# Attention's gating products and their lower pieces, moved from VectorE to GpSimd

## The chip, the cores and the metric

The kernel runs on one core of one Trainium2 chip. A core has five engines, each with its own instruction queue that it works off in order: TensorE (PE in the profile; its weight loads are PEld) multiplies matrices into PSUM, VectorE (DVE) and ScalarE (ACT) do element-wise work, GpSimd (POOL) does element-wise work on SBUF, and SyncE (SP) issues DMA transfers; ScalarE and GpSimd issue some of them too. [...] The metric is the time of one execution on the device, in microseconds (us); lower is better.

## What is computed

A decoder trunk of two layers on 1024 tokens of width 1024, in float32. Each layer normalises x, projects it to 5376 columns, runs two token mixers side by side, merges them by sigmoid gates and adds the projected result to x:

```python
h = rms_norm(x, norm_w[layer])
proj = h @ w_in[layer]
(q, k, v, z_attn, q_h, f_h, i_h, g_h, gate_attn, gate_hgrn) = jnp.split(proj, split_points, axis=-1)
...
a = sliding_window_attention(q, k, v, attn_sinks[layer]).astype(x.dtype) * jax.nn.silu(z_attn)
...
o = hgrn2_recurrence(heads(qin), heads(kin), heads(i_h.astype(jnp.float32)), heads(logf))
...
merged = (jax.nn.sigmoid(gate_attn) * (a @ w_up_attn[layer])
          + jax.nn.sigmoid(gate_hgrn) * (b @ w_up_hgrn[layer]))
x = x + merged @ w_out[layer]
```

The change concerns the product `* jax.nn.silu(z_attn)` in the line of `a`, and the preparation of `a` for `a @ w_up_attn`.

## The kernel before

Large matrix products are made in three: an operand is split into an upper piece, which is the value rounded to the matmul format fp32r, and a lower piece, which is what the rounding left. ScalarE makes the upper piece with a cast, and VectorE subtracts it from the value to get the lower piece. `split_w` does this into tiles that are used in turn, `split_slot` into tiles of the large pool (lines 380 to 385: the cast is L383, the subtraction L384). `split_w` already has an argument that names the engine of the subtraction; at the start of the kernel it is GpSimd for one chunk of weights.

A layer runs in stages. First come the projections in pairs (`pair`), then attention by blocks of 128 queries with the value projections of the recurrence beside it. Attention's output goes to DRAM (`ad`), and so does silu of its gate (`zd`). Then comes the stage of the heads, around which this case turns. The recurrence has four heads, and each is a generator (`core`) of ten steps: products that double a range (`grow`, with L946 on the query side Q and L955 on the key side R, both on VectorE), small matmuls into PSUM (`lv` L992 and L933, `l` L1044 and L1050, `lv_m` L1057), VectorE's merging of these into `acc`, GpSimd's copies of `acc` into the score tile `scT` (L1070), transposes (`tn` L1080), the states (`kv` L1092, then a chain of VectorE updates of R, L1096 and L1098) and the output (`po` L1109 and L1111). ScalarE copies the output to `tab` (L1112) and sums its squares (L1114), VectorE turns these sums into a scale (`ms_o` L116 and the lines up to L130) and applies it (L1116). `finish_head` transposes the result (`tb` L1125), multiplies it by its gate and splits it.

Between the steps of the heads the loop at the end of the stage advances a second generator, `filling`. It has TensorE project the forget gates and queries of heads 1 to 3 (`pj_f`, `pj_qh`), two chunks of weights a head, in halves, and then the upper projection of attention, `up_attn` (`pu_ua`, lines 147 to 149). After the halves 6, 7, 8 and 9 it calls `gate_attn`, once for each quarter of `a` (two halves of the tokens by two pairs of 128 channels). One call loads a quarter of the gate (`zr`) and of attention's output (`ar` in the profile) from DRAM with two DMAs on SyncE's queue (L1139), multiplies them on VectorE (L1140), and splits the product: cast on ScalarE (L383, `wh_a`), subtraction on VectorE (L384, `wl_a`). `up_attn` uses all four quarters as moving operands. SyncE's queue also holds the loads of weights (`wr`, `wr_ua`), which wait until one of three buffers comes free, and those of the heads (`f`, `R`, `Q`).

The order of the instructions in each engine's queue is not the order of the text. A planner sets it when the kernel is built: it estimates when each instruction's operands are ready, and fills each engine with what is ready first, by the place in the text among several. So a projection may stand between two steps of a head, and an instruction may be set at the head of a queue before its operand has in fact arrived, because the planner took the transfer to be done sooner. A few edges (`keep_in_program_order`, `issue_after`) tie the order elsewhere; none lies in this stage.

Of the kernel before, what the change touches and what calls it, by code (L numbers as in the profile page):

```python
# [10 lines left out]
F32 = mybir.dt.float32  # L11
# [3 lines left out]
ALU = mybir.AluOpType  # L15
AX = mybir.AxisListType

P = 128
# [22 lines left out]
def trunk_kernel(ctx, tc, x, positions, norm_w, w_in, attn_sinks, hgrn_norm_w, w_up_attn,  # L41
# [3 lines left out]
    V, S, G, PE = nc.vector, nc.scalar, nc.gpsimd, nc.tensor  # L45
# [11 lines left out]
    def slot(shape, name, dt=F32):  # L57
        return sp.tile(shape, dt, tag="slot", name=name)
# [318 lines left out]
        wh, wl = chunk(w, c0, nm)  # L377
        colsA(wh, wl, hT, nm, use, [H0, H1])

    def split_slot(raw, nm, shape):  # L380
        hi = slot(shape, f"wh_{nm}", F32R)
        lo = slot(shape, f"wl_{nm}", F32R)
        S.copy(hi, raw)  # L383
        V.tensor_tensor(out=lo, in0=raw, in1=hi.bitcast(F32), op=ALU.subtract)  # L384
        return hi, lo

    def split_rows(w, c0, n, nm, first=0):


        g = 1024 // n  # L390
        res = {}
        for k in range(0, KT, g):
            raw = wp.tile([P, g, n], F32, tag="wraw", name=f"wr_{nm}_{k}", bufs=3)
            nc.sync.dma_start(raw, w[k * P:(k + g) * P, c0:c0 + n].rearrange("(k p) c -> p k c", p=P))
            hi, lo = (split_w if k < first else split_slot)(raw, f"{nm}_{k}", [P, g, n])
            for j in range(g):
                res[k + j] = (hi[:, j], lo[:, j])
        return res
# [121 lines left out]
    for L in range(DEPTH):  # L520
# [54 lines left out]
        if L == 0:  # L575
            hT, hF = HT("0"), Turned("0")
            rest = norm_turn_soon([y for b in range(2) for y in norm_scale(xns[b:b + 1], None, f"n0_{b}", False, True)],
                                  hT, hF, 0, "n0_0", wt)
            aw = [split_w(raws[j], f"p0_{j}", [P, KT, P], G if j else V) for j in range(2)]
            aw += [split_slot(raws[j], f"p0_{j}", [P, KT, P]) for j in range(2, 4)]  # L580
            ys = list(norm_scale(xns[2:4], wb, "n0_2", True))
            for j in range(4):
# [275 lines left out]
        for u in range(NB):  # L858
            before(u)
            value(u)  # L860
            attend(u)
            if u == 5:
                w = [split_slot(load_chunk(wi, OF, f"f{L}_0"), f"f{L}_0", [P, KT, P])]
# [269 lines left out]
        def gate_attn(asp):  # L1133

            a = 0 if len(asp[0]) < 2 else 1
            j = len(asp[a])
            zr, t = (slot([P, 2, 512], f"{n}r_{L}_{a}_{j}") for n in ("z", "a"))
            for d, src in ((zr, zd), (t, ad)):
                nc.sync.dma_start(d, src[:, 2 * j:2 * j + 2, a * 512:(a + 1) * 512])  # L1139
            V.tensor_tensor(out=t, in0=t, in1=zr, op=ALU.mult)  # L1140
            asp[a].append(split_slot(t, f"a{L}_{a}_{j}", [P, 2, 512]))

        def filling():

            asp = [[], []]
            n = 0
            for h in range(1, NHG):
                for do, c in ((forget, OF), (query, OQH)):
                    w = chunk(wi, c + h * P, f"{c}_{L}_{h}")
                    for half in (H0, H1):  # L1150
                        do(h, w, [half])
                        yield
                        n += 1
                        if n in GATE:
                            gate_attn(asp)
            for m in range(0, KT, 2):
                for _ in up_attn(m, asp):
                    yield
# [35 lines left out]
        for m in range(0, KT, 2):  # L1194
# [5 lines left out]
            for a in range(2):  # L1200
                u, t = u2s[m // 2][a]
# [166 lines left out]
```

## Time and profile before

| what | value |
|---|---|
| time of the runs, median (lowest to highest of 3) | 1387.02 us (1384.45 to 1387.6) |
| the profiled execution's own time | 1387.23 us |
| its span on the core | 1385.5 us |
| TensorE busy | 98% of the span |
| VectorE, ScalarE, GpSimd busy | 72%, 51%, 8% |
| granted TensorE clock, mean | 0.996 |

The stage of the heads with its filling lies at about 430 to 575 us of the span for layer 0 and at about 1107 to 1256 us for layer 1.

The views are read as follows. A row of a group has the line, the engine, the operation, the tile written and the tiles read, the shapes and the count; in the view of a tile, the smallest, median and largest duration in ns and the first and last start. A row of the timeline has the start in us from the start of the span, the duration in us, the engine and the instruction; in brackets stands how long the engine sat idle before it and what ended that. Durations on one engine overlap slightly, since the next instruction starts while the last one drains. A row of the waits has the waiting engine and line, the one it waited for, the total in us, the count and the longest. A row of the stretches has start and end, length, busy time of PE, PEld, DVE, ACT and POOL with their instructions, the granted TensorE clock, the DMA engines' share and GB/s. Ends of matmuls are modelled, and spans on GpSimd are rough.

### The profile page before, as it was taken

To read this page: it belongs to the slowest core of one execution; us is meant where nothing else is said; L and a number is where in the kernel's file an instruction comes from. 1 tells how busy PE (TensorE), PEld (TensorE's weight loads), DVE (VectorE), ACT (ScalarE), POOL (GpSimd) and SP (SyncE) were. 2 spreads that over 40 slices of the span, in tenths; PEclk is the share of its full clock that TensorE was granted. 3 is DMA by queue.
4 is the path that set the end of the run, shared out by engine and by line. 5 is a ranking of instruction groups with operands and counts; after the bars stand their busy time and mean duration, and the time that the engine had idled before them with its cause. 6 is when DMAs were issued, how large, how long until landed. Compare 5 with 4: busy or idle time off the path is not lost.

```text
span 1385.5 us, 21538 instructions
## 1 busy us (share of the span) xinstructions
PE 1356.9 (98%) x8236; PEld 1127.0 (81%) x8236; DVE 997.3 (72%) x1638; ACT 708.8 (51%) x1418; POOL 109.2 (8%) x195
## 2 busy tenths in 40 slices
PE   7999999999999999999999999999999999999997
PEld 7888888888877888888888888887887788788885
DVE  6867668843646898599959666776356487867998
ACT  8844333443786655323666333344367766352254
POOL 1100012320000001000000001222100000100000
PEclk9999999999999999999999999999999999999999
DMA  9444476875225652860256336587913476329203
GB/s 290 165 134 145 137 225 204 264 262 212 92 95 189 231 189 76 310 239 29 86 181 189 126 125 194 173 259 217 335 49 107 142 236 217 108 85 402 91 1 122
DMA packets 204279, 240.06 MB, mean 173 GB/s; under 512 B 14288, under 2 KB 140752, under 8 KB 204176
## 3 DMA queue, kind: packets, MB, share of 16 engines
q1 hardware_dynamic: 156528, 145.08, 32.0%
q10 hardware_dynamic: 34944, 52.44, 10.4%
q0 software_dynamic: 12704, 41.17, 9.3%
q8 instruction: 65, 1.06, 0.3%
q14 instruction: 38, 0.31, 0.1%
HBM read 160.00 MB, written 78.64 MB: 172 GB/s over the span
## 4 chain that ended last, share of the span: by engine, by line
PE 80%; DVE 13%; ACT 3%; DMA 2%; issue 2%; SPq 0%; DVEq 0%; ACTq 0%
PE pb L308 6%; PE pb L310 6%; PE pb L309 6%; PE pc L308 4%; PE pc L310 4%; PE pc L309 4%; PE pg L270 3%; PE pg L272 3%; PE pg L271 3%; PE pu_uh L149 2%; PE pu_uh L147 2%; PE pu_uh L148 2%; PE pi L843 2%; PE pi L842 2%; PE pi L844 2%; PE av L816 2%
## 5 line engine op out<-in xcount | busy, mean ns | idle before, releaser
L136 ACT CAST whi_s<-ws 128x1024 fp32r<-128x1024 f32 x30 | 31.6, 1054 | 90.4 <-PE pc L310 89.0
L319 DVE TENSOR_TENSOR pq<-pc,pq 128x512 f32<-128x512 f32 x37 | 25.6, 691 | 61.4 <-PE pc L310 56.2
L136 ACT CAST whi_o<-wo 128x1024 fp32r<-128x1024 f32 x20 | 21.1, 1054 | 78.7 <-PE pu_uh L149 35.5
L544 ACT ACTIVATE pq<-pq 128x512 f32<-128x512 f32 x60 | 37.9, 631 | 43.9 <-DVE pq L319 42.3
L136 ACT CAST whi_t<-ws 128x1024 fp32r<-128x1024 f32 x30 | 31.6, 1054 | 41.8 <-PE pc L310 27.9
L147 PE MATMUL pu_ua<-wh_a,wlo_ua 128*128 128x512 f32 x128 | 52.2, 408 | 0.0
L780 ACT ACTIVATE pr<-pr,mx 128x128 f32<-128x128 f32 x128 | 49.6, 391 | 4.1 <-DVE mx L777 3.7
L149 PE MATMUL pu_ua<-wh_a,whi_ua 128*128 128x512 f32 x128 | 51.0, 399 | 0.0
L148 PE MATMUL pu_ua<-wl_a,whi_ua 128*128 128x512 f32 x128 | 50.3, 393 | 0.0
L147 PE MATMUL pu_uh<-wh_b,wlo_uh 128*128 128x512 f32 x128 | 49.8, 389 | 0.0
L148 PE MATMUL pu_uh<-wl_b,whi_uh 128*128 128x512 f32 x128 | 49.8, 389 | 0.0
L149 PE MATMUL pu_uh<-wh_b,whi_uh 128*128 128x512 f32 x128 | 49.8, 389 | 0.0
L270 PE MATMUL pg<-hh,wl_p 128*128 128x512 f32 (+1 forms) x128 | 46.9, 368 | 1.0 <-DVE wl_p L384 1.0
L308 PE MATMUL pb<-th,wl 128*128 128x512 f32 x120 | 47.2, 393 | 0.5 <-ACT pq L349 0.4
L308 PE MATMUL pb<-th,wlo_s 128*128 128x512 f32 x120 | 47.1, 392 | 0.0
L308 PE MATMUL pc<-hh,wlo_t 128*128 128x512 f32 x120 | 46.8, 390 | 0.0
L310 PE MATMUL pb<-th,wh 128*128 128x512 f32 x120 | 46.7, 389 | 0.0
L309 PE MATMUL pb<-tl,wh 128*128 128x512 f32 x120 | 46.7, 389 | 0.0
L310 PE MATMUL pc<-hh,whi_t 128*128 128x512 f32 x120 | 46.7, 389 | 0.0
L309 PE MATMUL pc<-hl,whi_t 128*128 128x512 f32 x120 | 46.7, 389 | 0.0
L310 PE MATMUL pb<-th,whi_s 128*128 128x512 f32 x120 | 46.7, 389 | 0.0
L309 PE MATMUL pb<-tl,whi_s 128*128 128x512 f32 x120 | 46.7, 389 | 0.0
(432 smaller groups left out, 4447.4 us busy)
## 6 DMA issues: line engine op xcount, KB each, us to landing
wr<-in_w_in_dram SPq DMA_DIRECT2D x72, 512.0 KB, 4.6
gd<-pq ACTq DMA_DIRECT2D x79, 256.0 KB, 3.0
fq<-fq ACTq DMA_DIRECT2D x48, 256.0 KB, 2.7
wr_p<-in_w_in_dram SPq DMA_DIRECT2D x23, 512.0 KB, 5.6
x<-in_x_dram SPq DMA_DIRECT2D x16, 512.0 KB, 6.3
qs<-qsd POOLq DMA_DIRECT2D x16, 512.0 KB, 7.5
u<-gd SPq DMA_DIRECT2D x16, 512.0 KB, 10.1
ga<-gd SPq DMA_DIRECT2D x16, 512.0 KB, 10.3
```

What stands on the lines that cost most here:

```text
L136: S.copy(hi, raw)
L147: PE.matmul(acc, lhsT=ll, rhs=rh, start=i == 0, stop=False)
L148: PE.matmul(acc, lhsT=lh, rhs=rl, start=False, stop=False)
L149: PE.matmul(acc, lhsT=lh, rhs=rh, start=False, stop=i == n - 1)
L270: PE.matmul(acc, lhsT=wl[:, k], rhs=h[:, t], start=k == 0, stop=False, skip_group_check=q > 0)
L271: PE.matmul(acc, lhsT=wh[:, k], rhs=l[:, t], start=False, stop=False, skip_group_check=q > 0)
L272: PE.matmul(acc, lhsT=wh[:, k], rhs=h[:, t], start=False, stop=k % 4 == 3, skip_group_check=q > 0)
L308: PE.matmul(acc, lhsT=wl[:, k], rhs=h, start=start and k == 0, stop=False, skip_group_check=not start)
L309: PE.matmul(acc, lhsT=wh[:, k], rhs=l, start=False, stop=False, skip_group_check=not start)
L310: PE.matmul(acc, lhsT=wh[:, k], rhs=h, start=False, stop=k == 3, skip_group_check=not start)
L544: S.activation(d, src, AF.Sigmoid if r < 2 * KT else AF.Silu)
L780: S.activation(pr[:, h], pr[:, h], AF.Exp, bias=mx[:, h:h + 1], accum_out=sm[:, h:h + 1])
```

## The change

`split_slot` gets an argument that names the engine of its subtraction, VectorE unless said otherwise. In `gate_attn` the product and the subtraction are given to GpSimd (`G`); `V` is VectorE and `S` ScalarE. The cast between them stays on ScalarE and the loads stay on SyncE. Eight products and eight subtractions are concerned, four of each in a layer. The other callers of `split_slot` are as before.

```diff
-    def split_slot(raw, nm, shape):
+    def split_slot(raw, nm, shape, eng=V):
         hi = slot(shape, f"wh_{nm}", F32R)
         lo = slot(shape, f"wl_{nm}", F32R)
         S.copy(hi, raw)
-        V.tensor_tensor(out=lo, in0=raw, in1=hi.bitcast(F32), op=ALU.subtract)
+        eng.tensor_tensor(out=lo, in0=raw, in1=hi.bitcast(F32), op=ALU.subtract)
         return hi, lo
...
             for d, src in ((zr, zd), (t, ad)):
                 nc.sync.dma_start(d, src[:, 2 * j:2 * j + 2, a * 512:(a + 1) * 512])
-            V.tensor_tensor(out=t, in0=t, in1=zr, op=ALU.mult)
-            asp[a].append(split_slot(t, f"a{L}_{a}_{j}", [P, 2, 512]))
+            G.tensor_tensor(out=t, in0=t, in1=zr, op=ALU.mult)
+            asp[a].append(split_slot(t, f"a{L}_{a}_{j}", [P, 2, 512], G))
```

## The prediction

> **What bounds the kernel now.** I read the page first: the engines' busy time and the list of the costliest groups. TensorE (PE) is busy 98% of the span, VectorE (DVE) 72%, GpSimd (POOL) 8%.
>
> ```profile
> span 1385.5 us, 21538 instructions
> PE 1356.9 (98%) x8236; PEld 1127.0 (81%) x8236; DVE 997.3 (72%) x1638; ACT 708.8 (51%) x1418; POOL 109.2 (8%) x195
> ```
>
> The profiled execution took 1387.23 us by its own clock, 1.73 us more than its span and 0.21 us above the median of 1387.02. I make the sum against 1387.23. A kernel that is 98% TensorE can gain only where TensorE waits, so the next view was that of TensorE's waits. Its largest row is the wait of the `lv` products (L992) for the doubling step of R (L955):
>
> ```profile
> PE lv L992 <- DVE R L955: 5.8, 2, 3.8
> PE tb L1125 <- DVE tab L1116: 3.4, 6, 0.9
> ```
>
> It is 5.8 us in two places, one in each layer. The timeline of TensorE gives both places, with the idle time ahead of them in brackets, and the `l` products (L1044) some 15 us earlier, which the chain below starts from:
>
> ```profile
> 477.91 0.39 PE L1111 MATMUL po<-R,Q 128*128 128x128 f32 x2
> 483.71 1.02 PE L1044 MATMUL l<-Q,R 128*32 128x64 f32 x29
> 501.38 0.64 PE L992 MATMUL lv<-f,ones 128*32 128x256 f32 x8 [2.07 <-DVE R L955]
> ...
> 1160.78 1.02 PE L1044 MATMUL l<-Q,R 128*32 128x64 f32 x29
> ```
> ```profile
> 1175.97 0.40 PE L148 MATMUL pu_ua<-wl_a,whi_ua 128*128 128x512 f32 x1
> 1180.14 1.08 PE L992 MATMUL lv<-f,ones 128*32 128x256 f32 x8 [3.77 <-DVE R L955]
> ```
>
> What TensorE waits for is VectorE, and VectorE had itself been standing still. Its timeline in layer 0, then in layer 1:
>
> ```profile
> 474.97 1.21 DVE L137 TENSOR_TENSOR wlo<-wr,whi 128x1024 fp32r<-128x1024 f32 x1
> 476.11 0.34 DVE L1098 SCALAR_TENSOR_TENSOR R<-R,tab,kv 128x128 f32<-128x128 f32 x1
> 483.59 1.23 DVE L1140 TENSOR_TENSOR ar<-ar,zr 128x1024 f32<-128x1024 f32 x1 [6.01 <-DMA ar<-ad]
> 485.93 1.22 DVE L384 TENSOR_TENSOR wl_a<-ar,wh_a 128x1024 fp32r<-128x1024 f32 x1 [1.11 <-ACT wh_a L383]
> 487.07 0.16 DVE L116 TENSOR_SCALAR ms_o<-so 128x8 f32<-128x8 f32 x1
> ...
> 500.63 0.69 DVE L955 TENSOR_TENSOR R<-R,tab 128x512 f32<-128x512 f32 x1
> ```
> ```profile
> 1162.36 1.23 DVE L1140 TENSOR_TENSOR ar<-ar,zr 128x1024 f32<-128x1024 f32 x1 [7.62 <-DMA ar<-ad]
> 1165.84 0.17 DVE L116 TENSOR_SCALAR ms_o<-so 128x8 f32<-128x8 f32 x1
> ...
> 1179.39 0.69 DVE L955 TENSOR_TENSOR R<-R,tab 128x512 f32<-128x512 f32 x1
> ```
>
> The fourth gating product (L1140) of each layer stands at the head of VectorE's queue for 6.01 and 7.62 us until its load lands. Then come the lower piece (L384) and a chain without a gap, from `ms_o` to the end of the R that TensorE waits for: 487.07 to 501.32 in layer 0 (14.25 us), 1165.84 to 1180.08 in layer 1 (14.24).
>
> The longer wait costs more than itself. In the table of stretches (start:end, length, busy time of PE, PEld, DVE, ACT, POOL, then the granted clock, DMA share, GB/s) the clock is 0.50 behind it, and 1.00 behind the 2.07 us of layer 0:
>
> ```profile
> 501.00:504.00 3.00, 2.62 (x92) 2.00 (x93) 3.00 (x6) 0.00 (x0) 0.00 (x0) 1.00 0.02 5
> ...
> 1180.00:1182.00 2.00, 1.86 (x76) 1.41 (x80) 2.00 (x5) 0.00 (x0) 0.00 (x0) 0.50 0.00 0
> 1182.00:1184.00 2.00, 2.00 (x25) 1.06 (x15) 2.00 (x4) 0.63 (x3) 0.00 (x0) 0.50 0.11 20
> 1184.00:1186.00 2.00, 2.00 (x7) 1.58 (x6) 2.00 (x6) 1.03 (x2) 0.00 (x0) 0.54 1.03 317
> ```
>
> Half the clock for three stretches of 2 us loses 1.0 + 1.0 + 0.9 = 2.9 us. So the two waits are worth 2.07 + 3.77 + 2.9 = 8.7 us, and this is the most that the change can win here.
>
> **The change, part by part: what leaves VectorE.** Eight products and eight lower pieces, in the view of the tile `ar`:
>
> ```profile
> L1140 DVE TENSOR_TENSOR ar<-ar,zr x8: 1215/1224/1254, 458.5 to 1162.4; 128x1024 f32<-128x1024 f32 x8
> ...
> L384 DVE TENSOR_TENSOR wl_a<-ar,wh_a x8: 1211/1221/1226, 461.4 to 1164.7; 128x1024 fp32r<-128x1024 f32 x8
> ```
>
> That is 8 x 1.224 + 8 x 1.221 = 19.6 us of VectorE's time, and the two stalls with it. The casts (L383) stay on ScalarE (ACT), between product and piece. What VectorE could start instead of stalling: the chain needs the `l` products (done at 483.71 + 1.02 = 484.73 and at 1161.80) and the sums of squares (L1114), which ScalarE makes eight of, 0.44 us apart:
>
> ```profile
> 480.99 0.32 ACT L1114 ACTIVATE f<-tab 128x128 f32<-128x128 f32 x1
> 481.43 0.31 ACT L1114 ACTIVATE f<-tab 128x128 f32<-128x128 f32 x1
> ...
> 484.85 1.05 ACT L383 CAST wh_a<-ar 128x1024 fp32r<-128x1024 f32 x1 [1.27 <-DVE ar L1140]
> ...
> 1158.15 0.32 ACT L1114 ACTIVATE f<-tab 128x128 f32<-128x128 f32 x1
> ```
>
> Without the cast among them they end at 480.99 + 8 x 0.44 = 484.5, and at 1161.7. The chain can then begin at about 485.0 for 487.07 (2.1 us sooner) and at 1161.8 for 1165.84 (4.0 us sooner). If nothing else changed, both waits would go.
>
> **What comes to GpSimd.** Sixteen two-input instructions of 128 x 1024. The trace has one such, in the start, and it lasts 2.73 us:
>
> ```profile
> 10.32 1.22 DVE L137 TENSOR_TENSOR wlo_p<-wr_p,whi_p 128x1024 fp32r<-128x1024 f32 x1
> ...
> 11.02 2.73 POOL L137 TENSOR_TENSOR wlo_p<-wr_p,whi_p 128x1024 fp32r<-128x1024 f32 x1 [10.13 <-ACT whi_p L136]
> ```
>
> As GpSimd's own work this is hidden: 16 x 2.73 = 44 us on an engine that is 8% busy. Queued behind it are only the copies into `scT` (L1070), and those of head 1, beside the fourth step, are read by `po` products that TensorE issues only after the `lv` of 501.38, so a few us of delay there cost nothing. The results are due late too: the upper projection that reads them begins at 498.6, where the last piece now starts at 485.93.
>
> ```profile
> L147 PE MATMUL pu_ua<-wh_a,wlo_ua x128: 387/389/628, 498.6 to 1255.5; 128*128 128x512 f32 x128
> ```
>
> But GpSimd and VectorE are not independent. Where four of those copies ran beside VectorE, its smallest two-input instruction took 0.37 us for 0.16:
>
> ```profile
> 519.55 0.16 DVE L128 TENSOR_TENSOR yt_o<-y_o 128x8 f32<-128x8 f32 x1
> 521.19 0.37 DVE L128 TENSOR_TENSOR yt_o<-y_o 128x8 f32<-128x8 f32 x1
> ...
> 520.76 3.74 POOL L1070 COPY scT<-acc 32x256 f32<-32x256 f32 x4 [29.38 <-DVE y_o L130]
> ```
>
> One copy of 256 elements a partition thus holds VectorE for 0.2 us. For a product, which reads 2 x 1024, that gives 8 x 0.2 = 1.6 us by size; the record of 2.73 us is the other bound; the lowest is no hold at all. I take 2.2 us: the one record is of the same operation and shape, and its first 0.52 us (11.02 to 11.54) lie under VectorE's L137, so its own part is 2.73 - 0.52 = 2.21. [...]
>
> **The sum.** Layer 0, with the load landing where it did: the product holds the port from 483.58 to 485.79, of which 0.8 us lie past 485.0, and the lower piece, behind the cast, holds 2.2 us inside the chain. The chain ends at 485.0 + 0.8 + 2.2 + 14.25 = 502.25, 0.9 us later than now; TensorE's wait becomes 3.0 us. Layer 1: both holds lie in the chain, 1161.8 + 4.4 + 14.24 = 1180.44, 0.4 us later; the wait becomes 4.1 us and the half clock stays. Together +1.3 us: 1388.5. What the stall gave away, the holds give away again. With holds of 1.6 us, layer 0 gains 0.3 and layer 1 gains 0.8, and its wait of 3.0 us may no longer cost the clock (2.9): -4.0, 1383.2. With 2.73, layer 0 loses 1.9 and its wait of 4.0 now costs 2.9 of clock, layer 1 loses 1.5: +6.3, 1393.5. This case's own range is 1383 to 1394. The first three steps of each layer I cost at nothing: behind them VectorE had its stall of 6 us, which takes up their holds, and TensorE's order, which the planner makes anew from its estimate of when things are ready, has projections to put ahead of what is late. Where that cover fails is the second rival.
>
> One more queue: the fourth pair of loads sits on SP behind a weight load that waits for its buffer, which L137 at 474.97 frees.
>
> ```profile
> 477.22 0.47 SPq L1139 DMA_DIRECT2D ar<-ad  x1
> ```
>
> If L137 moves, the landing moves with it; later puts both holds fully into layer 0's chain too (at most 1.4 us more), earlier takes the product's out of it.
>
> **Rivals.** First, the holds fall into VectorE's gaps or TensorE's order is remade around them: then only the stall's removal is left, -8.7 at most: 1378.5, and 1384 with a third of it. For: the planner slips L992 into the middle of a projection's accumulation, straight behind its L148 at 1175.97, so it fills TensorE up to the moment at which it expects R, and GpSimd's waiting for a load no longer upsets that. Against: the 0.2 us per copy.
>
> Second, on the other side: the holds of the first three steps reach TensorE. Three products and two pieces stand ahead of the last state update (L1098, done at 476.45), which `po` at 477.91 needs: 1.46 us of slack. Five holds of 2.2 are 11.0 us, 5 x 1.22 = 6.1 leave, so VectorE is 4.9 us late and TensorE waits 3.4 in each layer: 1.3 + 6.9, about 1395.5; with holds of 2.73 over 1400. It decides from a hold of (6.1 + 1.46) / 5 = 1.5 us on, if TensorE's order stays. For: in the 27 us before, VectorE is busy for 26.66, so a hold there finds no gap. Against: the order need not stay.
>
> ```profile
> 450.00:477.00 27.00, 27.00 (x221) 22.71 (x220) 26.66 (x46) 16.15 (x24) 2.67 (x4) 1.00 0.59 205
> ```
>
> Third, the change does not do what it says: the cast keeps its place among the sums of squares, and ScalarE waits for the load in VectorE's stead. GpSimd's product ends 2.73 us after the landing instead of 1.22, so `ms_o` comes 1.5 us later than now, and the piece holds 2.2 more: +3.7 in each layer, and layer 0's wait of 5.8 us then costs the clock (2.9) too: 1397.5.
>
> **How the numbers follow.** The likeliest is the balance: chance 0.40, 1388.5. The first rival has 0.31, the second 0.22, the third 0.07. A measurement of this kernel can tell about 0.2% (2.8 us) from no change. Of the balance's 0.40, 0.09 lie below 1384.4, 0.21 within, 0.10 above. So faster 0.31 + 0.09 = 0.40, same 0.21, slower 0.10 + 0.22 + 0.07 = 0.39. The range reaches from the first rival's end to the second's: 1379 to 1400.
>
> **What would show it.** Right: no wait of VectorE for `ar`; GpSimd's L1140 and L384 at 2.2 to 2.8 us or longer; VectorE instructions beside them longer by up to 2.2 us; the waits at L992 near 3 and 4 us. First rival: those waits gone and the clock at 1.00 throughout. Second: a new row of TensorE's waits, `po` or `l` for VectorE, and more total wait than 5.8 us. Third: ScalarE waiting for POOL's `ar` ahead of L1114. It is wrong altogether if VectorE's instructions keep their lengths beside GpSimd's.

## The result, and the profile after

The changed kernel takes 1407.89 us (median of 4 runs, 1407.23 to 1408.92) against 1386.24 for the kernel before in the same session: a ratio of 1.015, interval 1.013 to 1.017. It is slower by 21.7 us between the medians, outside the range of 1379 to 1400, where the likeliest case said 1388.5.

The page of the changed kernel, its first lines:

```profile
span 1406.4 us, 21558 instructions
PE 1367.1 (97%) x8236; PEld 1136.0 (81%) x8236; DVE 1006.8 (72%) x1622; ACT 710.2 (50%) x1418; POOL 150.1 (11%) x211
```

The same 8236 matmuls are busy for 10.2 us longer (1367.1 for 1356.9), and the remaining 10.7 of the 20.9 us of longer span are idle time. The 10.2 us are mostly clock: by the granted mean (0.987 for 0.996) it took some 18 us of the span for 6 before. About 3 of these us lie in the kernel's start, which the change doesn't touch (0.50 from 11 to 17 us here, 1.00 before), and so are not its doing. VectorE has 16 instructions less to do and is busy for 9.5 us longer; with the 19.6 us that left it, its other instructions take 29.1 us longer, 1.8 for each instruction on GpSimd. The view of TensorE's waits says where the idle time lies ("issue" stands where the profile names nothing that the engine waited for):

```profile
PE tb L1125 <- DVE tab L1116: 7.1, 7, 2.7
PE po L1111 <- DVE R L1096: 5.9, 2, 3.0
PE lv L992 <- issue: 5.9, 2, 3.8
...
PE po L1111 <- DVE R L1098: 1.0, 2, 0.6
PE tb L1125 <- ACT fq L703: 0.7, 1, 0.7
```

Before, `lv` had 5.8 us and `tb` 3.4. The `lv` waits that the change was to remove are no shorter (6.4 us), `po` is new with 6.9 us, and `tb` has grown by 4.4. The view of the tile `ar` has the moved instructions on GpSimd, at the length that the prediction expected:

```profile
L1140 POOL TENSOR_TENSOR ar<-ar,zr x8: 2372/2574/2850, 458.1 to 1180.4; 128x1024 f32<-128x1024 f32 x8
...
L384 POOL TENSOR_TENSOR wl_a<-ar,wh_a x8: 2379/2404/2956, 461.6 to 1184.3; 128x1024 fp32r<-128x1024 f32 x8
```

Now GpSimd's timeline in layer 0, then VectorE's beside it:

```profile
472.75 2.95 POOL L384 TENSOR_TENSOR wl_a<-ar,wh_a 128x1024 fp32r<-128x1024 f32 x1 [6.39 <-ACT wh_a L383]
475.67 2.79 POOL L1140 TENSOR_TENSOR ar<-ar,zr 128x1024 f32<-128x1024 f32 x1
479.61 2.41 POOL L384 TENSOR_TENSOR wl_a<-ar,wh_a 128x1024 fp32r<-128x1024 f32 x1 [1.16 <-ACT wh_a L383]
490.78 2.37 POOL L1140 TENSOR_TENSOR ar<-ar,zr 128x1024 f32<-128x1024 f32 x1 [8.76 <-DMA ar<-ad]
```
```profile
473.36 2.89 DVE L955 TENSOR_TENSOR R<-R,tab 128x512 f32<-128x512 f32 x1
476.17 2.83 DVE L946 TENSOR_TENSOR Q<-Q,tab 128x512 f32<-128x512 f32 x1
478.93 0.28 DVE L1096 COPY R<-kv 128x128 f32<-128x128 f32 x1
...
480.75 2.35 DVE L137 TENSOR_TENSOR wlo<-wr,whi 128x1024 fp32r<-128x1024 f32 x1
483.02 1.10 DVE L1098 SCALAR_TENSOR_TENSOR R<-R,tab,kv 128x128 f32<-128x128 f32 x3
...
498.16 0.17 DVE L116 TENSOR_SCALAR ms_o<-so 128x8 f32<-128x8 f32 x1 [3.65 <-ACT f L1114]
```

The doubling steps L955 and L946, 0.69 us before, take 2.89 and 2.83 us. Each is done 0.55 us, about its own length, behind the end of the GpSimd instruction beside it: 476.25 behind 472.75 + 2.95 = 475.70, and 479.00 behind 475.67 + 2.79 = 478.46. So it stood still until then. The hold is 2.1 to 2.2 us, as estimated. The state chain behind them (L1096, L1098) ends at 484.12 for 476.45, and so do things queued with it: the subtraction L137, whose buffer the fourth pair of loads waits behind, starts at 480.75 for 474.97, and that load lands in time for a product at 490.78 instead of 483.59. The loads of `f`, `R` and `Q` for the next head are queued behind it on SyncE and are late with it (`Q` is issued at 488.07 for 479.91).

TensorE meets this twice in layer 0, with its clock in the table of stretches (columns as in the prediction):

```profile
479.26 0.80 PE L1111 MATMUL po<-R,Q 128*128 128x128 f32 x2 [2.94 <-DVE R L1096]
483.41 0.79 PE L1111 MATMUL po<-R,Q 128*128 128x128 f32 x2 [0.37 <-DVE R L1098]
...
510.81 1.08 PE L992 MATMUL lv<-f,ones 128*32 128x256 f32 x8 [3.76 <-issue]
```
```profile
477.00:479.00 2.00, 0.00 (x0) 0.00 (x0) 2.00 (x2) 1.36 (x2) 1.46 (x1) 0.85 0.34 131
479.00:481.00 2.00, 1.74 (x8) 1.74 (x9) 1.93 (x7) 1.97 (x3) 1.39 (x1) 0.50 0.00 0
481.00:483.00 2.00, 2.00 (x10) 1.75 (x9) 2.00 (x1) 2.00 (x4) 1.02 (x1) 0.50 0.02 4
483.00:485.00 2.00, 1.63 (x8) 1.59 (x8) 1.05 (x4) 0.83 (x2) 0.00 (x0) 0.50 0.57 149
```

Six us at half the clock behind a wait of 2.94 us lose another 3. The `lv` wait that the view puts down to "issue" ends 0.11 us behind VectorE's L955 (510.02 + 0.68 = 510.70), so it is for R as before. And ScalarE's timeline has the fourth cast at the head of its queue, with seven of the eight sums of squares behind it, which is what `ms_o` at 498.16 waited for:

```profile
486.18 0.31 ACT L1114 ACTIVATE f<-tab 128x128 f32<-128x128 f32 x1
...
493.19 1.05 ACT L383 CAST wh_a<-ar 128x1024 fp32r<-128x1024 f32 x1 [6.61 <-POOL ar L1140]
494.14 0.30 ACT L1114 ACTIVATE f<-tab 128x128 f32<-128x128 f32 x1
```

So two theories lay ready. **H, the hold**: GpSimd's two-input instructions stop VectorE's for 2.2 us each, and VectorE is late by itself. **A, the queue**: ScalarE stands at the cast until the load has come, and the chain behind `ms_o` starts late.

### The profile page after: what moved, and what is told of

It reads as the page before. It is cut to its first block, busy times and chain, and to the rows that moved or that the text cites. A ratio compares the mean times of both kernels' runs of the same rounds, so it can differ in the third digit from the quotient of the medians.

```text
span 1406.4 us, 21558 instructions
## 1 busy us (share of the span) xinstructions
PE 1367.1 (97%) x8236; PEld 1136.0 (81%) x8236; DVE 1006.8 (72%) x1622; ACT 710.2 (50%) x1418; POOL 150.1 (11%) x211
## 3 DMA queue, kind: packets, MB, share of 16 engines
q10 hardware_dynamic: 34944, 52.44, 10.2%
## 5 line engine op out<-in xcount | busy, mean ns | idle before, releaser
L136 ACT CAST whi_o<-wo 128x1024 fp32r<-128x1024 f32 x20 | 21.1, 1054 | 78.7 <-PE pu_uh L149 35.5
L946 DVE TENSOR_TENSOR Q<-Q,tab 128x512 f32<-128x512 f32 x40 | 32.7, 817 | 27.5 <-PE l L1044 27.3
L1070 POOL COPY scT<-acc 32x256 f32<-32x256 f32 x32 | 21.5, 672 | 241.5 <-DVE acc L1067 125.2
## 6 DMA issues: line engine op xcount, KB each, us to landing
u<-gd SPq DMA_DIRECT2D x16, 512.0 KB, 10.2
ga<-gd SPq DMA_DIRECT2D x16, 512.0 KB, 10.2
```

Of the source, the lines that this page charges most:

```text
L946: return [V.tensor_tensor(out=Qv[:, :, 1], in0=Qv[:, :, 1], in1=Fv[:, :, 0:1].broadcast_to([P, n, hh]), op=ALU.mult)]
```

## The experiments

Each kernel's own time stands against runs of the kernel before on the same chip (medians of 1385 to 1387). PE's busy time and its waits are those of the one profiled execution, from each kernel's page and view of waits. Where an edit adds lines, the same instruction has another number (the product is L1140 to L1142, or L1148).

| kernel | median us | ratio to before (interval) | PE busy | waits `po` / `lv` / `tb` |
|---|---|---|---|---|
| before | 1386.24 | 1 | 1356.9 | 0 / 5.8 / 3.4 |
| after | 1407.89 | 1.015 (1.013 to 1.017) | 1367.1 | 6.9 / 6.4 / 7.8 |
| product_only | 1398.16 | 1.0098 (1.0081 to 1.0114) | 1359.3 | 2.0 / 7.7 / 6.6 |
| piece_only | 1390.56 | 1.0037 (1.0023 to 1.0051) | 1358.0 | 1.4 / 6.1 / 4.5 |
| first_three | 1404.10 | 1.0127 (1.0104 to 1.0149) | 1364.7 | 6.7 / 7.8 / 4.9 |
| last_only | 1392.94 | 1.0050 (1.0038 to 1.0063) | 1358.7 | 0 / 9.7 / 4.5 |
| idle_reads | 1409.88 | 1.0183 (1.0164 to 1.0202) | 1366.1 | 6.3 / 11.7 / 3.5 |
| idle_writes | 1391.41 | 1.0044 (1.0028 to 1.0061) | 1357.7 | 0 / 7.0 / 3.5 |
| after_cast_late | 1407.60 | 1.0153 (1.0131 to 1.0174) | 1364.5 | 7.4 / 7.8 / 5.8 |
| after_defer_look | 1407.55 | 1.0155 (1.012 to 1.019) | 1367.9 | 6.9 / 0.5 / 12.4 |
| after_early1 | 1403.57 | 1.0119 (1.0096 to 1.0143) | 1361.5 | 13.6 / 0 / 4.8 |
| before_early1 | 1380.86 | 0.9963 (0.9950 to 0.9977) | 1354.8 | 0 / 0.3 / 5.0 |
| before_poolq | 1380.81 | 0.9955 (0.9942 to 0.9969) | 1356.7 | 0 / 1.8 / 3.1 |

**Half of the change.** The pieces, or the products, go back to VectorE:

```diff
-            asp[a].append(split_slot(t, f"a{L}_{a}_{j}", [P, 2, 512], G))
+            asp[a].append(split_slot(t, f"a{L}_{a}_{j}", [P, 2, 512]))
```

> Only the eight products go to GpSimd; the lower pieces stay on VectorE. Theory H (each GpSimd instruction that reads two tiles holds VectorE's two-input instructions for 2.2 us, and the late state updates, late loads and waits follow from that): half the holds, so about half of the change's 21 us, 1394 to 1400. Theory A (what costs is ScalarE's cast, which waits 6.6 us for the fourth product with the sums of squares behind it): the product is on GpSimd as in the change, so nearly all of it, 1403 to 1408.

For piece_only it is the product that stays on VectorE:

```diff
-            G.tensor_tensor(out=t, in0=t, in1=zr, op=ALU.mult)
+            V.tensor_tensor(out=t, in0=t, in1=zr, op=ALU.mult)
```

> Only the eight lower pieces go to GpSimd; the products stay on VectorE and wait for their loads there, as before. H: half the holds again, 1392 to 1400. A: the cast waits for VectorE as before, so hardly any cost, 1385 to 1389.

The products alone cost 0.98%, the pieces alone 0.37%. The first lies in H's range; the second, 1390.56 us, lies between the two ranges. Each half costs, and their sum (1.35%) is near the whole (1.5%), but the loss doesn't go with the number of GpSimd instructions, which is eight in both. VectorE's other instructions take about as much longer in both (13.3 and 14.6 us by the pages), so it matters where the holds fall. In product_only ScalarE also stands for 5.40 us (layer 0) at the fourth cast, with seven sums of squares behind it, and in piece_only it doesn't, so this pair does not part H from A.

**Dead work on GpSimd.** The kernel before, with VectorE keeping all its work, and with two products a step on GpSimd whose results nobody reads; then, in the second run, with five memsets into a tile that nobody reads any more. The output is unchanged.

```diff
+            for e in range(2):
+                G.tensor_tensor(out=slot([P, 2, 512], f"d_{L}_{a}_{j}_{e}"), in0=zr, in1=zr, op=ALU.mult)
             V.tensor_tensor(out=t, in0=t, in1=zr, op=ALU.mult)
```

> The kernel before, with two GpSimd multiplications of the gate's tile by itself added in each step; nothing uses their results, and VectorE keeps all of its work. H: sixteen holds of 2.2 us and no relief of 19.6 us, so as slow as the change or slower, 1402 to 1425, with TensorE waiting for VectorE at po and lv. A: nothing of the path changes, 1385 to 1390.

```diff
             V.tensor_tensor(out=t, in0=t, in1=zr, op=ALU.mult)
+            for e in range(5):
+                G.memset(zr, 0.0)
```

> The kernel before, with five GpSimd memsets of the gate's tile (0.95 us each, as long together as the two multiplications) added behind each product; they write only. H, if the hold is the port for reads: no hold, 1385 to 1390. If any GpSimd work beside VectorE slows it, as slow as the added multiplications.

The reads cost 1.8%, though nothing reads their results and the fourth cast stands behind the sixth sum of squares, as in the kernel before: H, without help from A. With the same 1638 instructions VectorE is busy for 1017.4 us instead of 997.3. Their timeline on GpSimd, then VectorE's instructions beside the pair at 473.96, which take 0.45 and 0.40 us in the changed kernel (at 471.13 and 471.83), where GpSimd is idle:

```profile
473.96 3.93 POOL L1141 TENSOR_TENSOR d<-zr 128x1024 f32<-128x1024 f32 x2 [8.49 <-DMA zr<-zd]
```
```profile
474.36 1.78 DVE L1023 TENSOR_TENSOR f<-Q,tab 128x256 f32<-128x256 f32 x1
476.06 2.11 DVE L1023 TENSOR_TENSOR gs<-Q,tab 128x256 f32<-128x256 f32 x1
```

The memsets keep GpSimd busy longer (5.0 us a step for 3.9) and cost 0.44%, a little above what H gave them; VectorE is busy for 999.0 us. Their trace shows a part of the reason:

```profile
475.33 4.99 POOL L1142 MEMSET zr<- 128x1024 f32 x5 [2.50 <-issue]
486.00 5.00 POOL L1142 MEMSET zr<- 128x1024 f32 x5 [5.67 <-DVE ar L1140]
```
```profile
475.39 1.22 DVE L137 TENSOR_TENSOR wlo<-wr,whi 128x1024 fp32r<-128x1024 f32 x1
476.79 1.22 DVE L384 TENSOR_TENSOR wl_a<-ar,wh_a 128x1024 fp32r<-128x1024 f32 x1
...
488.25 0.75 DVE L116 TENSOR_SCALAR ms_o<-so 128x8 f32<-128x8 f32 x1
489.03 0.98 DVE L124 TENSOR_SCALAR yi_o<-ms_o 128x8 int32<-128x8 int32 x1
```

The two-input L137 and L384 keep their 1.22 us beside a memset. The three TENSOR_SCALARs of the chain, 0.17 us before, take up to 0.98, about one memset each. The chain starts 1.2 us later, behind a load that lands later (VectorE's product is at 484.71), and takes 1.1 us longer, and the `lv` wait of layer 0 grows from 2.07 to 3.98 us. So in these two traces VectorE's two-input instructions took longer beside GpSimd's products (2.11 us for 0.40) and not beside its memsets (1.22 us for 1.22), while its TENSOR_SCALARs took longer beside the memsets (0.98 us for 0.17). What the two engines share, a port or something else, no run shows.

**Which steps.** First the three early steps of each layer on GpSimd with the fourth on VectorE, then the fourth alone:

```diff
+            eng = G if (a, j) != (1, 1) else V
-            G.tensor_tensor(out=t, in0=t, in1=zr, op=ALU.mult)
-            asp[a].append(split_slot(t, f"a{L}_{a}_{j}", [P, 2, 512], G))
+            eng.tensor_tensor(out=t, in0=t, in1=zr, op=ALU.mult)
+            asp[a].append(split_slot(t, f"a{L}_{a}_{j}", [P, 2, 512], eng))
```

> Products and pieces of the first three gating steps of each layer on GpSimd, of the fourth on VectorE. The prediction costed these three steps at nothing; by it this kernel takes about as long as before, 1385 to 1389, since VectorE's stall at the fourth product takes up their holds. By H the holds of three products and two or three pieces reach TensorE at po: waits of about 3 us in each layer with half clock behind them, and the chain to the lv products still starts behind the fourth load: 1394 to 1404.

```diff
-            eng = G if (a, j) != (1, 1) else V
+            eng = G if (a, j) == (1, 1) else V
```

> Only the product and the piece of the fourth gating step of each layer on GpSimd, the first three on VectorE. No po waits by either theory. The prediction's sum for this step alone: waits of 3.0 and 4.1 us at L992 for 2.07 and 3.77, thus 1387 to 1391. If the cast stands early among the sums of squares and ScalarE waits for the load, both waits reach the length that costs the clock: 1391 to 1397. If the stall's removal wins, as it does with earlier loads, 1379 to 1383.

The three steps that the prediction costed at nothing cost 1.27%, most of the whole, at the upper end of H's range. TensorE's waits in first_three, and VectorE at the fourth product, now its own again:

```profile
PE lv L992 <- issue: 7.5, 2, 3.8
PE po L1111 <- DVE R L1096: 6.0, 2, 3.0
```
```profile
491.01 1.23 DVE L1141 TENSOR_TENSOR ar<-ar,zr 128x1024 f32<-128x1024 f32 x1 [6.58 <-DMA ar<-ad]
```

The `po` waits are those of the changed kernel, and the stall that was to absorb the holds is there in full, 6.58 us: it moved back with its load, from 483.59 to 491.01. The cast has moved here too: ScalarE stands at it for 6.25 us behind the first sum of squares, so the `lv` waits of this kernel can't be put down to H alone.

The fourth step alone costs 0.5%, 1392.9 us, and no `po` wait; its `lv` waits are 3.9 and 5.8 us where the sum gave 3.0 and 4.1. Its trace has the second case of the expectation, on ScalarE and then on VectorE:

```profile
486.21 1.05 ACT L383 CAST wh_a<-ar 128x1024 fp32r<-128x1024 f32 x1 [2.80 <-POOL ar L1141]
```
```profile
489.37 0.41 DVE L116 TENSOR_SCALAR ms_o<-so 128x8 f32<-128x8 f32 x1 [2.04 <-ACT f L1114]
```

The cast stands behind the fifth sum of squares, ScalarE waits at it for GpSimd's product (4.76 us in layer 1), and VectorE's chain waits for the three sums that are left. There A has a part.

**ScalarE's cast.** The first attempt tied the fourth cast to its place in the program:

```diff
-        S.copy(hi, raw)
+        cast = S.copy(hi, raw)
+        if pin:
+            tc.keep_in_program_order(cast)
...
-            asp[a].append(split_slot(t, f"a{L}_{a}_{j}", [P, 2, 512], G))
+            asp[a].append(split_slot(t, f"a{L}_{a}_{j}", [P, 2, 512], G, pin=len(asp[0]) == 2 and j == 1))
```

> The changed kernel, with the fourth cast of each layer kept behind everything that stands ahead of it in the program on ScalarE, thus behind the eight sums of squares; the products and pieces stay on GpSimd. Two theories of the 21 us that the change lost. H, the hold: each GpSimd instruction with two inputs stops VectorE's two-input instructions for about 2.2 us, and VectorE comes late by itself. A, the queue: ScalarE stands at the fourth cast, with seven sums of squares behind it, for as long as GpSimd's product waits for its load (6.6 us in layer 0), and VectorE's chain to the lv products starts that much later. If A has a part, ms_o comes some 8 us sooner, the waits at L992 (5.9 us) and the half clock behind them go or shrink, and the time is 1394 to 1400; the po waits of 5.9 us stay. By H alone 1404 to 1409.

This did not move the cast. In its trace it stands behind the first sum of squares still:

```profile
492.40 1.05 ACT L383 CAST wh_a<-ar 128x1024 fp32r<-128x1024 f32 x1 [6.25 <-POOL ar L1142]
```

So it says nothing on A. The second puts the fourth cast and piece one fill step later:

```diff
-            asp[a].append(split_slot(t, f"a{L}_{a}_{j}", [P, 2, 512], G))
+            if (a, j) != (1, 1):
+                asp[a].append(split_slot(t, f"a{L}_{a}_{j}", [P, 2, 512], G))
+            else:
+                later.append(t)
...
+                        if n == GATE[3] + 1:
+                            asp[1].append(split_slot(later.pop(), f"a{L}_1_1", [P, 2, 512], G))
                         if n in GATE:
                             gate_attn(asp)
```

> The changed kernel, with the cast and the lower piece of the fourth gating step of each layer put one fill step later in the program, so that on ScalarE the cast follows all eight sums of squares; all products and pieces stay on GpSimd and the loads where they were. This is the test of A that the pinned cast was meant to be. If A has a part, VectorE's wait for f ahead of ms_o goes, ms_o comes at about 490 instead of 498.16, and the waits at L992 (5.9 us) with the half clock behind them (about 6 us) go or shrink: 1394 to 1401. By H alone, in which the lv products are late because VectorE was held, 1404 to 1409. The po waits of 5.9 us stay in both.

Its median was 1408.15 us. A second run of the same kernel gives the trace that is read here:

> The same kernel as after_defer, for a trace that is not disturbed (the first one ran at 0.63 of the clock throughout). Its time of 1408.2 says that A has no part in the end. If A fell because the cast no longer blocks but something else takes its place, the row of ms_o names it: VectorE's wait ahead of ms_o is for another engine (PE's l or pj_f, or a DMA), at about the same moment, 496 to 499. If the chain starts sooner, near 492, and the lv waits are gone, the lost time must stand at another place, most likely more po or tb waits.

ScalarE no longer stands at the cast, the `lv` waits are gone, and the time has not moved. In TensorE's waits and VectorE's timeline:

```profile
PE tb L1125 <- DVE tab L1116: 12.4, 8, 3.7
PE po L1111 <- DVE R L1096: 5.9, 2, 3.0
```
```profile
495.76 1.23 DVE L967 TENSOR_TENSOR gs<-R,Q 128x1024 f32<-128x1024 f32 x1 [10.40 <-DMA Q<-fq]
...
497.51 2.37 DVE L116 TENSOR_SCALAR ms_o<-so 128x8 f32<-128x8 f32 x1
```

VectorE now does the head's doubling steps first and `ms_o` within them, held for 2.37 us by the fourth piece (0.16 before), and the scale of L1116 comes late for `tb` instead. Ahead of both it stands for 10.40 us, for the load of `Q`. That load is queued on SyncE behind the same weight load that waits for L137: L137 starts at 481.97 for 474.97, and `Q` is issued at 487.56 for 479.91. So taking A away gains nothing in this kernel, because another stall, which the holds cause, is there in its place; what A would cost alone is not shown by it.

**The loads.** The pair of loads of each step is issued one fill step earlier, in the changed kernel and in the kernel before; and in the kernel before from GpSimd's queue instead of SyncE's, at the same step.

```diff
+        loaded = []
+        def gate_load(i):
+            a, j = divmod(i, 2)
+            zr, t = (slot([P, 2, 512], f"{n}r_{L}_{a}_{j}") for n in ("z", "a"))
+            for d, src in ((zr, zd), (t, ad)):
+                nc.sync.dma_start(d, src[:, 2 * j:2 * j + 2, a * 512:(a + 1) * 512])
+            loaded.append((zr, t))
...
+                        if n + 1 in GATE:
+                            gate_load(n + 1 - GATE[0])
```

> The changed kernel, with the two loads of each gating step issued one fill step earlier, so that they have landed when GpSimd and ScalarE come to them. A: no wait of ScalarE for GpSimd's product of more than about 3 us, the waits at L992 gone or under 2 us: 1394 to 1400, as with the cast behind the sums of squares. H: the holds and with them the po waits (5.9 us and the half clock behind them) stay in any case, so not under 1392; by H alone 1402 to 1409.

> The kernel before, products and pieces on VectorE, with the loads of each gating step issued one fill step earlier. This takes VectorE's stalls of 6.0 and 7.6 us away without a single GpSimd instruction. If these stalls cost what the prediction said (2.07 + 3.77 us of wait and 2.9 us of half clock), 1377 to 1380, faster by 0.4 to 0.7%. If TensorE's wait moves to another place, or the earlier loads take their buffers or queue slots from the weight loads, 1384 to 1390.

For before_poolq the call comes at `n` and the issue is:

```diff
-                nc.sync.dma_start(d, src[:, 2 * j:2 * j + 2, a * 512:(a + 1) * 512])
+                nc.gpsimd.dma_start(d, src[:, 2 * j:2 * j + 2, a * 512:(a + 1) * 512])
```

> The kernel before, with the loads of the gating steps issued from GpSimd's queue, at the same step, so that they do not stand behind a weight load on SyncE's queue. If the fourth pair's landing is late because of that queue, it lands some 7 us sooner, VectorE's stalls go, and the time is 1377 to 1380. If it is late because it is issued late (its buffer, or the order on GpSimd) the stalls stay: 1384 to 1388.

Without a GpSimd instruction on the data, both ways of loading sooner make the kernel faster, by 0.37% and 0.45% (about 5 to 6 us), the fastest here, though just short of the 1377 to 1380 that was expected. In before_early1 the last issue of the four pairs is at 463.40 (SyncE's queue), 13.8 us before the 477.22 of the kernel before, and TensorE's wait for `lv` is gone:

```profile
463.40 0.42 SPq L1140 DMA_DIRECT2D ar<-ad  x1
```
```profile
PE tb L1125 <- DVE tab L1116: 5.0, 6, 1.6
...
PE lv L992 <- issue: 0.3, 2, 0.2
```

With the GpSimd work, the same earlier loads leave 1403.6 us. The `lv` waits go there too, but the fourth product and piece now fall ahead of `po` like the other three:

```profile
PE po L1111 <- DVE R L1096: 7.0, 2, 3.6
PE po L1111 <- DVE R L1098: 6.6, 4, 1.8
```

This pair has no stall at the fourth gating load and no cast that waits among the sums of squares, and what is left between its two kernels is GpSimd's sixteen instructions, with the order that the planner makes around them: 1403.57 - 1380.86 = 22.7 us.

## Why the prediction was wrong

The cause is H: idle_reads and the pair with early loads lose 22 to 25 us without A. The prediction had the size of a hold right, 2.2 us, with GpSimd's instructions at 2.4 to 3.0 us. That it is a port that is held, as its sum has it, no run shows; what the runs showed is longer VectorE instructions beside GpSimd's, 2.89 and 2.83 us for 0.69. What failed is where the holds fall.

**The step that failed** is "The first three steps of each layer I cost at nothing: behind them VectorE had its stall of 6 us, which takes up their holds, and TensorE's order [...] has projections to put ahead of what is late." Neither cover was there. A stall covers only what is due after it, and `po` (477.91 before) is due ahead of the stall's end at 483.59. Nor does the stall stay in place: it ends with a load that is queued behind L137, a VectorE instruction which the holds delay. In first_three it is still 6.58 us long, 7.4 us later. The prediction saw that the landing moves with L137 and allowed at most 1.4 us for it; in the changed kernel `ms_o` starts 11.1 us later (498.16 for 487.07). And no projection was put between the holds and `po`, so the lateness met TensorE.

**The second rival** was therefore the nearest: "VectorE is 4.9 us late and TensorE waits 3.4 in each layer". The changed kernel waits 2.94 + 0.37 = 3.3 us in layer 0. That the two agree is partly luck. The third piece has come ahead of `po` too, the first update of R (L1096) is 9.0 us late (478.93 for 469.94), and the last (L1098) 7.7; but the first `po` products that read R had 5 us to spare, and behind them TensorE runs at half clock. The rival's price of 1395.5 left out two terms. The half clock was counted at `lv` alone; behind `po` it costs 3 us more in layer 0 (three stretches of 2 us at 0.50). And what comes after `po` was taken to be unchanged, whereas the load came 7.2 us later (490.78 for 483.59) and with it the whole chain to `lv` and `tb`. Summed over the kernel, TensorE's waits at these three places went from 9.2 to 21.1 us and its busy time grew by 10.2 us.

**The third rival** gave the mechanism of ScalarE's wait right but for the cast's place: it moved up from behind the sixth sum to behind the first, and the wait was 6.61 us. In after_defer_look this wait is gone and the time is the same, with VectorE's stall for `Q` in its place.

**The balance** at the fourth step, taken alone, was sized too low: last_only gives 1392.9 where the sum gave 1388.5, because its `lv` waits came to 9.7 us for 7.1, and layer 0's 3.9 costs the clock as well (0.50 from 504 to 506 us). The sum took the cast out from among the sums of squares and let the chain begin at 485.0; in last_only the cast stood behind the fifth, and `ms_o` began at 489.37. Here the mechanism of the third rival, which had the lowest chance, is what happened, though not to its size of 1397.5. The lower bound of a hold, 1.6 us, was misread as well: the copy beside the 0.37 us ran from 520.76 to 521.54, so the 0.2 us were what was left of the copy when VectorE came to it, and not its whole hold.

**The stall itself** was rightly read: taking it away by earlier loads wins 5 to 6 us, two thirds of the 8.7 that were called the most.

Left open is how the loss splits between the `lv` and the `tb` chain in the changed kernel, since they trade places from one kernel to the next. Nor does a run hold the planner's order fixed: each edit has it remade, and what that alone costs is not shown (idle_writes, whose twenty memsets a layer are new to it too, loses 0.44% in all). Whether smaller GpSimd instructions in VectorE's few gaps would cost less wasn't tried.

## What to carry to other kernels

Before moving an elementwise instruction to GpSimd to spare VectorE, ask what VectorE does beside it: here, where that read two tensors from SBUF, it lost up to 2.2 us to a GpSimd instruction of 128x1024 (1.8 on average) to save 1.2. Such a move can only win where VectorE is idle for that long and nothing due earlier waits behind it. Where an engine stalls at the head of its queue for a load, move the load: here that won most of what the change could win, without it. And an idle stretch of an engine covers lateness only of work due behind it, and only if what ends it is not itself delayed.

## What the runs showed of the hardware

Whether a TensorE wait costs the clock does not follow from its length. The `po` wait of 2.94 us was followed by 6 us at half clock, and the `lv` wait of 3.76 us in layer 1 of product_only by none; of the two `po` waits of 2.32 us in idle_reads, the first by none (until 480.16) and the second by almost 7 us at half clock (until 1170.14, 0.50 from 1172.26 on).

What the traces show in its place is a grid. Within one trace the stretches of half clock begin whole multiples of 3.41 us apart (478.42 and 509.14 us in the changed kernel, nine steps), and nearly all last one or two steps. Here are the two steps around the `po` wait of the changed kernel, then the wait of product_only and its steps:

```profile
475.01:478.42 3.41, 1.31 (x8) 0.97 (x6) 3.41 (x2) 1.56 (x2) 3.41 (x2) 1.00 0.20 77
478.42:481.83 3.41, 2.57 (x12) 2.57 (x13) 3.34 (x7) 3.31 (x5) 2.25 (x2) 0.50 0.00 0
```
```profile
1191.80 0.64 PE L992 MATMUL lv<-f,ones 128*32 128x256 f32 x8 [3.76 <-issue]
```
```profile
1186.57:1189.98 3.41, 1.47 (x14) 1.23 (x12) 3.41 (x5) 1.08 (x2) 0.00 (x0) 1.00 0.10 37
1189.98:1193.39 3.41, 1.59 (x88) 1.37 (x88) 3.38 (x7) 0.00 (x0) 0.00 (x0) 1.00 0.49 159
1193.39:1196.80 3.41, 3.41 (x27) 2.71 (x17) 3.41 (x7) 1.75 (x4) 0.00 (x0) 1.00 0.35 114
```

The shorter wait left TensorE idle for 2.10 us of one step, and the next was at half clock; the longer one was divided, 1.94 and 1.82 us, and no half clock followed. In all these traces but that of after_defer, from 18 us on and without the last 12 us, 29 steps at full clock held 2.05 us or more of idle TensorE, and half clock followed each of them; of those with 1.94 us or less it followed one (1.58 us, in idle_reads). The grid does not lie at the same place in every trace: in the kernel before a half clock begins at 1179.03 us, 205.3 steps from the 478.42 of the changed kernel. So it may be in part chance which waits cost the clock, and a half clock in one trace need not be there in the next execution; that is an estimate, from the granted mean of the kernel before, which went from 0.993 to 0.998 from run to run.

The `po` wait of 2.94 us, shorter than a whole step of 3.41 us, was enough in the changed kernel. The prediction's list of what costs the clock held only the 3.77 us of `lv`.

GpSimd instructions that only write were not free for VectorE either: in idle_writes, beside memsets of 1.00 us, its TENSOR_SCALARs went from 0.17 us to between 0.75 and 0.98, while its two-input L137 and L384 kept their 1.22.
